# Samples' state products on two row quarters of the array, with their x rows spread by DMA

## The chip, the cores and the metric

The kernel runs on one core of one Trainium2 chip. Its time is the device time of one execution in microseconds (us); where several executions are given, the time is their median. The engines are named as the profile names them: PE is the matrix engine (PEld its loading of weights), DVE the vector engine, ACT the scalar engine, POOL the general-purpose engine, SP the engine that here only issues DMAs.

## The reference

The program is one inference step of a one-layer decoder. A layer has a mixer (a chunked gated MLP beside a Mamba-2 state-space model, SSD) and a convolutional feed-forward net. It works on 256 tokens of a new sequence (the prompt) and on 8 other sequences (the samples) of 8 new tokens each, 320 tokens in all. The part that the change touches is the samples' recurrence:

```
h_t = exp(dt_t a) h_{t-1} + dt_t x_t B_t^T,   y_t = h_t C_t
states = jnp.einsum("bcsgn,bcsgr,bcsgrp->bcgrpn", bc, decay_states, xdt)
...
ssm_state_sample  (DEPTH, DEC_BATCH, SSM_HEADS, SSM_HEAD_DIM, SSM_STATE)
```

There are 32 heads of 64 channels in 4 groups (8 heads each); a group shares B and C, which have 128 state entries. For each of the 8 samples and each of the 4 groups, the new state (128 x 512 numbers: state entries by the 8 heads' channels) is the old one, shrunk by a factor per head, plus the product of B (8 tokens x 128) with the decayed x (8 tokens x 512).

## The kernel before

All large products are projections: weights of 128 x 1024 numbers (a slab, 512 KB) come from memory by SP's DMAs, ACT rounds them to a high part `whi`, DVE subtracts that to get a low part `wlo`, and PE makes three products for each 128 x 128 block (`accumulate`, lines 131 to 137): high with high, high weights with the low part of the data, low weights with the high part. The moving side is always the 320 tokens. Both parts have the type fp32r, a rounded fp32.

The SSD work is cut into small steps. `ssd(g)` (from line 896) is a generator for group g = 0 to 3. A planner (`tick`, `advance`, lines 147 to 175) calls its next step between slabs of the projections, after a number of products that the step itself asked for with `yield`. So the SSD's matmuls stand in PE's order between slabs, at places fixed when the program is built; for groups 0 to 3 that is the stretch from about 415 to 800 us. The small matmuls write into a ring of four PSUM banks, `misc`.

The samples are handled in two halves, i = 0, 1 of four sequences each (32 tokens), and for each group in these steps:

- `fourfold` (line 427) makes on ACT `x4`, a copy of the samples' x with each half repeated four times along the tokens. `x_of_samples` (line 932) transposes it on PE, four transposes for each half, so that 128 rows hold 32 tokens four times over. `ps_x` are the two results.
- `samples_split` (line 938) multiplies by dt times the decay (`times`, DVE), ACT rounds the product into `xsp`, and DVE replaces rows 64 to 127 by what the rounding left over. `samples_rows` (line 944) takes other rows of the same transposes for the outputs y.
- `bsp` holds B in the same manner: four copies of 32 tokens, two of them high parts and two low parts, so that the sum over 128 rows gives all four products of high and low parts.
- `picked` (line 992) makes for each i of 0 to 3 on ACT a masked copy `bm` of `bsp`, in which only the rows of the i-th sequence of each half are kept; the mask is `bsel`.
- `shrunk` (line 997) multiplies the old states by their factor on POOL. `grown` (line 1003) makes, for the i-th sequence of each half h, one product of `bm[:, h]` with `xsp[:, h]` over all 128 rows (128 x 512), and DVE adds it to the state. `end` (line 1024) does that and stores the state. `ends` says in which steps: 2, 5, 7 and 10; for group 3 the last one is done behind all projections of the mixer (line 1125).

Thus there are 4 groups x 4 values of i x 2 halves = 32 of these products, in 16 pairs. PE's products for the state that goes in (`with_c`, `ps_yo`) and for the outputs (`products`, `y_ps`) use parts of the array, 32 or 64 of its columns side by side, by `tile_position`; the products of `grown` use it whole.

Of the kernel before, what the change touches and what calls it, by code (L numbers as in the profile page):

```python
# [33 lines left out]
def hybrid_step(  # L34
# [37 lines left out]
    bd2 = cp.tile([P, P], F32, name="bd2")  # L72
    bsel = cp.tile([P, 4], F32, name="bsel")
    upper_s = cp.tile([P, NS], F32, name="upper_s")
# [3 lines left out]
    def masks():  # L78
        make_upper_triangular(nc, upper, 1.0, diag=True)
        make_lower_triangular(nc, later, 1.0, diag=False)  # L80
        make_block_diagonal(nc, bd2, TS)

        for r in range(4):
            rs = slice(32 * r, 32 * r + 32)
            pool.tensor_copy(bsel[rs], bd2[rs, rs].rearrange("p (b t) -> p b t", b=4)[:, :, 0])
# [340 lines left out]

    def fourfold(out, x, i):

        act.copy(out.rearrange("p k (q t) -> p k q t", q=4), x[:, :, NP + 32 * i:NP + 32 * i + 32].unsqueeze(2).to_broadcast([P, 4, 4, 32]))
        return out  # L430

    with ExitStack() as mctx:
# [68 lines left out]
        def steps():  # L501
# [82 lines left out]
            act.activation(dec.rearrange("p c h -> p (c h)"), ps_dec[:, :H5], AF.Exp)  # L584
            dve.tensor_tensor(out=dt[:, 3:5], in0=dt[:, 3:5], in1=dec[:, 3:5], op=ALU.mult)

            sp.dma_start(tote, tot_d.unsqueeze(0).broadcast_to([P, NH, NB]))
# [3 lines left out]
        with tc.tile_pool(name="gp", bufs=1) as gp:  # L591
# [252 lines left out]
            for g in range(4):  # L844
                res = []
                mix = gate_mix(g, uf, res)
                bg.append(mix)
                if g < 3:
                    uf = gate_up(g + 1)
                    if g == 2:  # L850
                        b4 = [[tp.tile([P, NT], F32, tag="pv", name="b4", bufs=4)[:, :256] for _ in range(2)] for _ in range(2)]
                        for i in range(2):
                            o = NP + 32 * i
                            for h in range(2):
                                pool.dma_start(b4[i][h], b_d[o:o + 32, 256 * h:256 * h + 256].unsqueeze(0).broadcast_to([4, 32, 256]))
                    finish(mix)
                    chunk_out(w_out, g, *res, g == 0)
# [4 lines left out]
        with tc.tile_pool(name="sd", bufs=1) as sd:  # L862
# [3 lines left out]
            shared = op.tile([P, NT + NS + 2 * P], F32, tag="dtf", name="cb_cms", bufs=1)  # L866
            cb, cms = shared[:, :NT + NS], shared[:, NT + NS:].rearrange("p (b i) -> p b i", b=NB)
            pool.tensor_copy(cb[:NS, :NS], ident[:NS, :NS])
# [12 lines left out]
            def load_state(g, i):  # L881

                st = [sd.tile([P, 512], F32, tag="st", name="st", bufs=6) for _ in range(2)]
                for h in range(2):
                    sp.dma_start(st[h], state_ssm[4 * h + i, g])
                return st
# [9 lines left out]
            def ssd(g):  # L896
# [16 lines left out]
                for h in range(2):  # L913
                    sp.dma_start(st3[h], state_ssm[4 * h + 3, g])
# [16 lines left out]

                def x_of_samples(i):
                    ps = misc("xt_ps")
                    for j in range(4):
                        by_token(ps[:, P * j:P * j + P], x4[:, i, P * j:P * j + P], 0)
                    return ps

                def samples_split(i, ps):
                    xq = sd.tile([P, 512], F32, tag="xde", name="xq", bufs=2)
                    times(xq, ps, 3 + i)  # L940
                    act.copy(xsp[:, i], xq)
                    dve.tensor_tensor(out=xsp[64:, i], in0=xq[64:], in1=xsp[64:, i].bitcast(F32), op=ALU.subtract)

                def samples_rows(i, ps):
                    for r in range(2):
                        at = slice(64 - 64 * r + 32 * i, 96 - 64 * r + 32 * i)
                        times(xdt[at, 2, 256 * r:256 * r + 256], ps[at, 256 * r:256 * r + 256], 2, at, slice(4 * r, 4 * r + 4))

# [28 lines left out]

                ps_x = [x_of_samples(i) for i in range(2)]
                ps_s = misc("s1_ps")
# [4 lines left out]
                def with_c(i, st):  # L984

                    for r in range(2):
                        for h in range(2):
                            row = 64 * r + 32 * h
                            pe.matmul(ps_yo[row:row + 32, :256], cms[:, 4 * h + i, :], st[h][:, 256 * r:256 * r + 256],  # L989
                                      start=i == 0, stop=i == 3, tile_position=(0, row))  # L990

                def picked(i):
                    bm = sd.tile([P, 2, P], F32R, tag="bm", name="bm", bufs=2)
                    act.activation(bm, bsp[:, :, bs].bitcast(F32), AF.Copy, scale=bsel[:, i:i + 1])
                    return bm

                def shrunk(i, st):
                    with first():
                        for h in range(2):
                            pool.tensor_tensor(out=by_head(st[h]), in0=by_head(st[h]),  # L1000
                                               in1=tote[:, h0:h0 + 8, 4 * h + i:4 * h + i + 1].to_broadcast([P, 8, 64]), op=ALU.mult)

                def grown(st, bm):
                    for h in range(2):
                        ps = misc("up_ps")
                        made = pe.matmul(ps, bm[:, h], xsp[:, h], start=True, stop=True)  # L1006
                        with first():
                            dve.tensor_tensor(out=st[h], in0=st[h], in1=ps, op=ALU.add)
                    return made.ins

                def store_state(i, st, by=act):
                    for h in range(2):
                        by.dma_start(o_ssm_s[4 * h + i, g], st[h])

# [6 lines left out]

                bms = {}

                def end(i, by=act):
                    made = grown(sts[i], bms.pop(i))
                    store_state(i, sts[i], by)
# [56 lines left out]
                ends = {2: 0, 5: 1, 7: 2, 10: 3}  # L1083
                picks = {0: (0, 1), 2: (2,), 5: (3,)}
                shrinks = {0: 0, 2: 1, 5: 2, 8: 3}
# [4 lines left out]
                for n in range(13 - e):  # L1090
                    if n == 0:
                        samples_split(1, ps_x[1])
                    if n == 1:
                        for i in range(2):
                            samples_rows(i, ps_x[i])
# [3 lines left out]
                    for i in picks.get(n, ()):  # L1099
                        bms[i] = picked(i)  # L1100
                    if n in (6, 12 - e):
# [431 lines left out]
```

## Time and profile before

| | |
|---|---|
| time, median of 3 runs | 1751.21 us (1750.23 to 1751.52) |
| time of the profiled execution | 1750.2 us |
| its span, first to last instruction | 1748.5 us |
| granted PE clock | 0.999 |
| PE / PEld / DVE / ACT / POOL busy | 1740.9 / 1720.8 / 1181.3 / 822.2 / 316.8 us |
| DMA | 302.54 MB, 173 GB/s on average |

"Busy" for PE counts matmuls, which are pipelined: the next one starts while the one before still drains, so what a matmul costs is the time from its start to the next one's start (its slot), not its duration. A row of the timeline gives the start, the duration of the row's instructions together, the engine, the line, the operation, what it writes and reads, the part of the array (rows*columns), the moving data's shape, and how many instructions the row merges. An fp32 matmul stands as two instructions, one of fp32r and a transpose as one.

### The profile page before, as it was taken

The numbers are of one execution on the slowest core, as the hardware profiler recorded it, in microseconds if no ns is written. First come the engines' busy times: TensorE is split into PE (matmuls) and PEld (weight loads), VectorE is DVE, ScalarE is ACT, GpSimd is POOL, SyncE is SP. The second block draws the span as 40 slices with busy tenths as digits, with TensorE's granted clock in tenths as the row PEclk, the third lists the DMA queues.
The fourth block names the chain that finished last, engine by engine and source line by source line (L and its number), as shares of the span: only waits on it lengthen the run. The fifth ranks groups of instructions, "written<-read, shape, count | busy, mean of one in ns | idle before, by whom it ended". The sixth has DMA issues, their size and how long they took to land.

```text
span 1748.5 us, 31128 instructions
## 1 busy us (share of the span) xinstructions
PE 1740.9 (100%) x12075; PEld 1720.8 (98%) x12075; DVE 1181.3 (68%) x2015; ACT 822.2 (47%) x1202; POOL 316.8 (18%) x682
## 2 busy tenths in 40 slices
PE   9999999999999999999999999999999999999998
PEld 9999999999999999999999999999999999999997
DVE  7558864667969787778855566565657565656577
ACT  6344544334656565646545434343434343333345
POOL 2532230000423323111210101010201010101002
PEclk9999999999999999999999999999999999999999
DMA  8786565556576676664655555455554545555543
GB/s 262 223 233 182 183 176 157 154 166 195 189 227 206 198 232 194 213 191 151 190 156 152 154 148 157 146 155 150 155 150 149 155 149 149 157 149 155 146 159 109
DMA packets 227747, 302.54 MB, mean 173 GB/s; under 512 B 21392, under 2 KB 152080, under 8 KB 227408
## 3 DMA queue, kind: packets, MB, share of 16 engines
q1 hardware_dynamic: 210976, 272.42, 51.8%
q0 software_dynamic: 6176, 13.87, 2.6%
q10 hardware_dynamic: 10448, 14.26, 2.3%
q8 instruction: 95, 1.56, 0.4%
q14 instruction: 52, 0.43, 0.1%
HBM read 280.54 MB, written 19.69 MB: 172 GB/s over the span
## 4 chain that ended last, share of the span: by engine, by line
PE 98%; DVE 1%; ACT 1%; issue 0%; POOLq 0%; ACTq 0%
PE ps L134 21%; PE ps L135 20%; PE ps L136 20%; PE pd L134 10%; PE pd L136 10%; PE pd L135 10%; PE y_ps L1070 1%; PE ps_v L135 1%; PE ps_v L134 1%; PE ps_v L136 1%; PE yo_ps L989 0%; PE up_ps L1006 0%; PE sg L812 0%; PE xt_ps L412 0%; DVE wlo L124 0%; ACT whi L123 0%
## 5 line engine op out<-in xcount | busy, mean ns | idle before, releaser
L124 DVE TENSOR_TENSOR wlo<-wraw,whi 128x1024 fp32r<-128x1024 f32 (+2 forms) x480 | 583.0, 1215 | 416.7 <-ACT whi L123 414.0
L123 ACT CAST whi<-wraw 128x1024 fp32r<-128x1024 f32 (+2 forms) x479 | 495.7, 1035 | 688.7 <-PE ps L135 393.9
L134 PE MATMUL ps<-h_hi,whi 128*128 128x320 f32 x2428 | 750.1, 309 | 0.0
L135 PE MATMUL ps<-h_lo,whi 128*128 128x320 f32 x2428 | 748.5, 308 | 0.0
L136 PE MATMUL ps<-h_hi,wlo 128*128 128x320 f32 x2428 | 747.9, 308 | 0.0
L134 PEld LDWEIGHTS ps<-h_hi,whi 128*128 128x128 f32 x2428 | 455.5, 188 | 3.1 <-issue 1.8
L135 PEld LDWEIGHTS ps<-h_lo,whi 128*128 128x128 f32 x2428 | 455.7, 188 | 0.4
L136 PEld LDWEIGHTS ps<-h_hi,wlo 128*128 128x128 f32 x2428 | 455.5, 188 | 0.0
L136 PE MATMUL pd<-fhi,wlo 128*128 128x320 f32 x704 | 217.0, 308 | 0.0
L135 PE MATMUL pd<-flo,whi 128*128 128x320 f32 x704 | 217.0, 308 | 0.0
L134 PE MATMUL pd<-fhi,whi 128*128 128x320 f32 x704 | 217.0, 308 | 0.0
L134 PE MATMUL pd<-ohi,whi 128*128 128x320 f32 x448 | 138.8, 310 | 0.0
L136 PE MATMUL pd<-ohi,wlo 128*128 128x320 f32 x448 | 138.3, 309 | 0.0
L135 PE MATMUL pd<-olo,whi 128*128 128x320 f32 x448 | 138.3, 309 | 0.0
L136 PEld LDWEIGHTS pd<-fhi,wlo 128*128 128x128 f32 x704 | 132.1, 188 | 0.0
L134 PEld LDWEIGHTS pd<-fhi,whi 128*128 128x128 f32 x704 | 132.1, 188 | 0.0
L135 PEld LDWEIGHTS pd<-flo,whi 128*128 128x128 f32 x704 | 132.1, 188 | 0.0
L1318 POOL COPY ptf<-pad 128x2 f32<-128x2 f32 x88 | 21.0, 238 | 602.2 <-DVE pad L1306 601.5
L247 DVE TENSOR_TENSOR acc_ffn<-acc_ffn,pd 128x320 f32<-128x320 f32 (+1 forms) x161 | 77.1, 479 | 29.3 <-PE pd L136 28.0
L134 PEld LDWEIGHTS pd<-ohi,whi 128*128 128x128 f32 x448 | 84.1, 188 | 0.7
L135 PEld LDWEIGHTS pd<-olo,whi 128*128 128x128 f32 x448 | 84.1, 188 | 0.3
L136 PEld LDWEIGHTS pd<-ohi,wlo 128*128 128x128 f32 x448 | 84.1, 188 | 0.0
(342 smaller groups left out, 1728.4 us busy)
## 6 DMA issues: line engine op xcount, KB each, us to landing
wraw<-in_ffn_w_up SPq DMA_DIRECT2D x176, 512.0 KB, 3.7
wraw<-in_w_in SPq DMA_DIRECT2D x132, 512.0 KB, 4.0
wraw<-in_ffn_w_down SPq DMA_DIRECT2D x88, 512.0 KB, 3.4
wraw<-in_w_out SPq DMA_DIRECT2D x64, 512.0 KB, 3.5
st<-in_state_ssm SPq DMA_DIRECT2D x40, 256.0 KB, 4.3
out_ssm_state_sample<-st ACTq DMA_DIRECT2D x30, 256.0 KB, 3.0
cs<-dacs_d SPq DMA_DIRECT2D x16, 320.0 KB, 4.8
wraw<-in_w_in SPq DMA_DIRECT2D x12, 384.0 KB, 4.1
```

The costliest lines, as they stand in the source:

```text
L123: rounded[:] = [act.copy(hi, raw).ins]
L124: dve.tensor_tensor(out=lo, in0=raw, in1=hi.bitcast(F32), op=ALU.subtract)
L134: pe.matmul(ps, whi, xhi, start=first, stop=False)
L135: pe.matmul(ps, whi, xlo, start=False, stop=False)
L136: last_made[0] = pe.matmul(ps, wlo, xhi, start=False, stop=last).ins
L247: added_last[:] = [dve.tensor_tensor(out=acc[:, nb, ts], in0=acc[:, nb, ts], in1=ps[:, ts], op=ALU.add).ins]
L1070: pe.matmul(ps[64 * i:64 * i + 64, cols], w(hl), x(hl, m, cpx), tile_position=(0, 64 * i), **flags)
L1318: pool.tensor_copy(ptf[:, k, :], pad[:, 256:258])
```

## The change

The rows of `bsp` and `xsp` are put in another order. Before, the 128 rows of a half were four blocks, each with all 32 tokens; now they are 32 runs of four, each run for one token: two copies of high parts and two of low parts of B (`odd`, `sign` tell which rows), high and low parts of x in turn. So the 32 rows of a quarter of the array belong to one sequence of 8 tokens, and a product for that sequence needs only its quarter.

- The masks `bsel`, the masked copies `bm` and `picked` are gone (16 ACT instructions of 128 x 256).
- `grown` makes its two products first, each on 32 rows, on two different quarters ((i + h) mod 4), and then the two additions. `seq(h, i)` renumbers the sequences to fit; the loads and stores of states follow it.
- The fourfold copy is gone (8 ACT copies). `x_of_samples` makes four transposes straight from `xs`, of 64 columns each (all samples once), in place of eight of 128.
- `samples_split` works once on 64 rows: a multiplication on DVE, a rounding on ACT into rows 0 to 63 of the new tile `x_parts`, a subtraction on DVE into rows 64 to 127. `x_parts` takes a buffer of the ring `xde`.
- New: `strips` fills `xsp` from `x_parts` by four DMAs within SBUF for each group, each of 64 rows of 2 KB and repeating a row twice: the high parts from ACT's queue, the low parts from POOL's. The shrinking of the states 1 to 3 is ordered behind POOL's two DMAs (`issue_after(filled[1])`).
- `samples_rows` takes two DVE instructions of 64 rows in place of four of 32, in step 0 instead of 1.
- In `b_of_samples`, once: four ACT instructions with a scale per row, and eight DVE instructions over all rows in place of eight over 32 rows. The DMAs that bring B repeat each token four times instead of the block.
- Small things at the start: two DVE instructions make `odd` and `sign`; four POOL copies that made `bsel` are gone; one POOL copy joins the decays of the two halves in `dt`.

In PE's order every matmul keeps its place. In group 0, before (the rows are engine order, not time; `ps` and `pd` are slab products):

```order
L136 MATMUL ps_3_4579<-h_hi,wlo 128x320
L412 MATMUL xt_ps<-ident,x_4628 128x128 x8
L980 MATMUL s_ps<-xde,btok 128x512
L989 MATMUL yo_ps<-st,cb_cms 32x256 x12
...
L136 MATMUL pd_5_5091<-ohi,wlo 128x320
L1006 MATMUL up_ps<-xsp,bm 128x512 x2
L134 MATMUL pd_6_5123<-ohi,whi 128x320
```

and now:

```order
L134 MATMUL ps_3_4579<-h_hi,wlo 128x320
L933 MATMUL xt_ps<-ident,xs 64x128 x4
L989 MATMUL s_ps<-xde,btok 128x512
L998 MATMUL yo_ps<-st,cb_cms 32x256 x12
...
L134 MATMUL pd_5_5078<-ohi,wlo 128x320
L1012 MATMUL up_ps<-xsp,bsp 128x512 x2
L132 MATMUL pd_6_5108<-ohi,whi 128x320
```

Four transposes are left of eight, and the pair `up_ps` reads `bsp` itself; nothing else moved on PE.

On POOL, around the fill of group 1, before (`st` are states being shrunk, `xde` and `cpx` decayed copies for the outputs):

```order
L1120 TENSOR_TENSOR s_5793<-s_5793,dec 128x512
L928 TENSOR_TENSOR xde<-xdt,dec 128x512
L1000 TENSOR_TENSOR st<-st,tote 128x512 x6
L928 TENSOR_TENSOR xde<-xdt,dec 128x512
L1050 TENSOR_TENSOR cpx<-cpx,cT 128x256
```

and now:

```order
L1121 TENSOR_TENSOR s_5768<-s_5768,dec 128x512
L926 TENSOR_TENSOR xde<-xdt,dec 128x512
L1004 TENSOR_TENSOR st<-st,tote 128x512 x2
L948 DMA xsp<-x_parts 64x1x512 x2
L1004 TENSOR_TENSOR st<-st,tote 128x512 x4
L926 TENSOR_TENSOR xde<-xdt,dec 128x512
L1056 TENSOR_TENSOR cpx<-cpx,cT 128x256
```

The two DMAs stand between the first and the second pair of shrunk states; four of the six, `xde` and `cpx` come behind them.

The diff, cut to its core:

```diff
-                                pool.dma_start(b4[i][h], b_d[o:o + 32, 256 * h:256 * h + 256].unsqueeze(0).broadcast_to([4, 32, 256]))
+                                pool.dma_start(b4[i][h], b_d[o:o + 32, 256 * h:256 * h + 256].unsqueeze(1).broadcast_to([32, 4, 256]))
...
-                        act.copy(out, raw)
-                        for rs in (slice(32, 64), slice(96, P)):
-                            dve.tensor_tensor(out=out[rs], in0=raw[rs], in1=out[rs].bitcast(F32), op=ALU.subtract)
+                        act.activation(out, raw, AF.Copy, scale=sign)
+                        for k in range(2):
+                            dve.scalar_tensor_tensor(out=out[:, :, k], in0=raw[:, :, k], scalar=odd, in1=out[:, :, k].bitcast(F32),
+                                                     op0=ALU.mult, op1=ALU.add)
+            def seq(h, i):
+                return 4 * h + (i + h) % 4
...
-                x4 = sd.tile([P, 2, 512], F32, tag="xsp", name="x4", bufs=1)
-                for i in range(2):
-                    fourfold(x4[:, i].rearrange("p (k n) -> p k n", n=P), xs, i)
...
-                def x_of_samples(i):
+                def x_of_samples():
                     ps = misc("xt_ps")
                     for j in range(4):
-                        by_token(ps[:, P * j:P * j + P], x4[:, i, P * j:P * j + P], 0)
+                        pe.transpose(ps[:NS, P * j:P * j + P], xs[:, j, NP:NT], ident)
                     return ps
 
-                def samples_split(i, ps):
+                def samples_split(ps):
                     xq = sd.tile([P, 512], F32, tag="xde", name="xq", bufs=2)
-                    times(xq, ps, 3 + i)
-                    act.copy(xsp[:, i], xq)
-                    dve.tensor_tensor(out=xsp[64:, i], in0=xq[64:], in1=xsp[64:, i].bitcast(F32), op=ALU.subtract)
+                    parts = sd.tile([P, 512], F32R, tag="xde", name="x_parts", bufs=2)
+                    lower = slice(0, NS)
+                    times(xq[lower], ps[lower], 3, lower)
+                    act.copy(parts[lower], xq[lower])
+                    dve.tensor_tensor(out=parts[NS:], in0=xq[lower], in1=parts[lower].bitcast(F32), op=ALU.subtract)
+                    return parts
+
+                def strips(parts, half):
+                    for i in range(2):
+                        o = NS * half + 32 * i
+                        made = (pool if half else act).dma_start(xsp[half::2, i].bitcast(F32),
+                                                                 parts[o:o + 32].bitcast(F32).unsqueeze(1).broadcast_to([32, 2, 512]))
+                    return made.ins
...
-                def picked(i):
-                    bm = sd.tile([P, 2, P], F32R, tag="bm", name="bm", bufs=2)
-                    act.activation(bm, bsp[:, :, bs].bitcast(F32), AF.Copy, scale=bsel[:, i:i + 1])
-                    return bm
...
-                def grown(st, bm):
+                def grown(i, st):
+                    up = []
                     for h in range(2):
-                        ps = misc("up_ps")
-                        made = pe.matmul(ps, bm[:, h], xsp[:, h], start=True, stop=True)
+                        rs = slice(32 * ((i + h) % 4), 32 * ((i + h) % 4) + 32)
+                        up.append(misc("up_ps"))
+                        made = pe.matmul(up[h], bsp[rs, h, bs], xsp[rs, h], start=True, stop=True, tile_position=(rs.start, 0))
+                    for h in range(2):
                         with first():
-                            dve.tensor_tensor(out=st[h], in0=st[h], in1=ps, op=ALU.add)
+                            dve.tensor_tensor(out=st[h], in0=st[h], in1=up[h], op=ALU.add)
...
-                samples_split(0, ps_x[0])
+                x_parts = samples_split(ps_x)
+                filled = [strips(x_parts, half) for half in range(2)]
...
                     if n in shrinks:
-                        shrunk(shrinks[n], sts[shrinks[n]])
+                        with tc.issue_after(filled[1]) if n else nullcontext():
+                            shrunk(shrinks[n], sts[shrinks[n]])
```

More of the change, by code (lines that the diff above doesn't have):

```diff
@@ L72, in hybrid_step @@
     bd2 = cp.tile([P, P], F32, name="bd2")
-    bsel = cp.tile([P, 4], F32, name="bsel")
+    odd = cp.tile([P, 1], F32, name="odd")
+    sign = cp.tile([P, 1], F32, name="sign")
     upper_s = cp.tile([P, NS], F32, name="upper_s")
@@ L81, in masks @@
         make_block_diagonal(nc, bd2, TS)
-        for r in range(4):
-            rs = slice(32 * r, 32 * r + 32)
-            pool.tensor_copy(bsel[rs], bd2[rs, rs].rearrange("p (b t) -> p b t", b=4)[:, :, 0])
         for r in range(2):
@@ L867, in hybrid_step @@
             cb, cms = shared[:, :NT + NS], shared[:, NT + NS:].rearrange("p (b i) -> p b i", b=NB)
+            dve.tensor_reduce(out=odd, in_=ident.rearrange("p (t d h) -> p d t h", d=2, h=2)[:, 1], axis=mybir.AxisListType.XY, op=ALU.add)
+            dve.tensor_scalar(out=sign, in0=odd, scalar1=-2.0, scalar2=1.0, op0=ALU.mult, op1=ALU.add)
             pool.tensor_copy(cb[:NS, :NS], ident[:NS, :NS])
@@ L930, in decayed, with samples_rows @@
                     return xde
-                def x_of_samples(i):
+                def x_of_samples():
                     ps = misc("xt_ps")
                     for j in range(4):
-                        by_token(ps[:, P * j:P * j + P], x4[:, i, P * j:P * j + P], 0)
+                        pe.transpose(ps[:NS, P * j:P * j + P], xs[:, j, NP:NT], ident)
                     return ps
-                def samples_split(i, ps):
+                def samples_split(ps):
                     xq = sd.tile([P, 512], F32, tag="xde", name="xq", bufs=2)
-                    times(xq, ps, 3 + i)
-                    act.copy(xsp[:, i], xq)
-                    dve.tensor_tensor(out=xsp[64:, i], in0=xq[64:], in1=xsp[64:, i].bitcast(F32), op=ALU.subtract)
-                def samples_rows(i, ps):
+                    parts = sd.tile([P, 512], F32R, tag="xde", name="x_parts", bufs=2)
[10 more added lines that the diff above has]
+                    return made.ins
+                def samples_rows(ps):
                     for r in range(2):
-                        at = slice(64 - 64 * r + 32 * i, 96 - 64 * r + 32 * i)
-                        times(xdt[at, 2, 256 * r:256 * r + 256], ps[at, 256 * r:256 * r + 256], 2, at, slice(4 * r, 4 * r + 4))
+                        at, hs = slice(NS - NS * r, P - NS * r), slice(256 * r, 256 * r + 256)
+                        dve.tensor_tensor(out=by_head(xdt[at, 2, hs]), in0=by_head(ps[:NS, hs]),
+                                          in1=dt[:NS, 2, h0 + 4 * r:h0 + 4 * r + 4].unsqueeze(2).to_broadcast([NS, 4, 64]), op=ALU.mult)
                 for c in range(2):
@@ L976, in ssd @@
                 yield 48, 72
-                ps_x = [x_of_samples(i) for i in range(2)]
+                ps_x = x_of_samples()
                 ps_s = misc("s1_ps")
@@ L988, in with_c @@
                             row = 64 * r + 32 * h
-                            pe.matmul(ps_yo[row:row + 32, :256], cms[:, 4 * h + i, :], st[h][:, 256 * r:256 * r + 256],
+                            pe.matmul(ps_yo[row:row + 32, :256], cms[:, seq(h, i), :], st[h][:, 256 * r:256 * r + 256],
                                       start=i == 0, stop=i == 3, tile_position=(0, row))
-                def picked(i):
-                    bm = sd.tile([P, 2, P], F32R, tag="bm", name="bm", bufs=2)
-                    act.activation(bm, bsp[:, :, bs].bitcast(F32), AF.Copy, scale=bsel[:, i:i + 1])
-                    return bm
                 def shrunk(i, st):
@@ L1091, in ssd @@
                     if n == 0:
[L1092 to L1095, printed above, removed]
+                        samples_rows(ps_x)
                         yo_to_xdt()
```

18 lines of the change are left out of this document (6 added, 12 removed).

## The prediction

> **What bounds the kernel now.** I read the engines' busy times first, then the chain of work that ended last, then the table of who waited for whom, and last PE's timeline at the places that the change touches. From the page:
>
> ```profile
> PE 1740.9 (100%) x12075; PEld 1720.8 (98%) x12075; DVE 1181.3 (68%) x2015; ACT 822.2 (47%) x1202; POOL 316.8 (18%) x682
> ...
> PE 98%; DVE 1%; ACT 1%; issue 0%; POOLq 0%; ACTq 0%
> ```
>
> PE is busy all the time and is 98% of the chain. All that PE waited for in 1748.5 us (engine, line, what it waited for, us in total, times, longest):
>
> ```profile
> PE early L69 <- DVE ones L65: 1.1, 1, 1.1
> PE both L1423 <- ACT f_tok L1421: 1.0, 1, 1.0
> ```
>
> One wait is at the start, one at the end; between them PE runs through its fixed order without a gap. So a matmul is worth its slot, the time from its start to the next start, and work of ACT, DVE, POOL or the DMAs is worth nothing, unless PE comes to wait for it. The forecast is therefore a sum of PE slots in 16 pairs of state products and 4 sets of transposes.
>
> **The pairs before.** PE's timeline at the first pair (start, duration, engine, line, operation, part of the array, shape, how many):
>
> ```profile
> 459.84 0.31 PE L134 MATMUL pd<-ohi,whi 128*128 128x320 f32 x1
> 459.99 0.31 PE L135 MATMUL pd<-olo,whi 128*128 128x320 f32 x1
> 460.14 0.31 PE L136 MATMUL pd<-ohi,wlo 128*128 128x320 f32 x1
> 460.29 0.62 PE L1006 MATMUL up_ps<-xsp,bm 128*128 128x512 f32 x2
> 460.75 0.30 PE L134 MATMUL pd<-ohi,whi 128*128 128x320 f32 x1
> 460.89 0.31 PE L135 MATMUL pd<-olo,whi 128*128 128x320 f32 x1
> ```
>
> Slab products start every 0.147 us. From 460.14 to 460.89 are 0.75 us with the pair, and would be 0.29 without: a pair costs 0.46 us, 0.23 for each product of 512 columns.
>
> **The pairs after.** Each product now takes 32 of the 128 rows, so the array changes from whole to row quarters and back 16 times. The trace has no row quarter, but it has column parts and one half of the rows. Column parts, at group 0, with the sample transposes ahead of them:
>
> ```profile
> 435.22 0.31 PE L136 MATMUL ps<-h_hi,wlo 128*128 128x320 f32 x1
> 435.37 1.03 PE L412 MATMUL xt_ps<-ident,x 128*128 128x128 f32 x8
> 436.24 1.02 PE L980 MATMUL s_ps<-xde,btok 128*128 128x512 f32 x2
> ...
> 436.67 0.59 PE L980 MATMUL s_ps<-xde,btok 128*128 128x512 f32 x1
> 437.20 1.93 PE L989 MATMUL yo_ps<-st,cb_cms 128*32 128x256 f32 x32
> 439.06 0.41 PE L134 MATMUL ps<-h_hi,whi 128*128 128x320 f32 x1
> 439.31 0.31 PE L135 MATMUL ps<-h_lo,whi 128*128 128x320 f32 x1
> 439.46 0.31 PE L136 MATMUL ps<-h_hi,wlo 128*128 128x320 f32 x1
> ```
>
> (436.67 is the second of the two `s_ps` instructions, shown alone.) And half of the rows, 64*128, in the steps near 232 us:
>
> ```profile
> 232.60 0.39 PE L556 MATMUL dec_ps<-sp_e,ones 128*128 128x32 f32 x2
> 232.71 0.28 PE L556 MATMUL dec_ps<-sp_e,ones 128*128 128x32 f32 x1
> 232.92 0.29 PE L558 MATMUL dec_ps<-sp_e,sums_of 64*128 64x32 f32 x1
> ```
>
> What a change of parts costs:
>
> - Going in: the second `s_ps` instruction holds PE for 0.53 us (436.67 to 437.20), the first for 0.43: 0.10 us. For rows the same: 0.21 (232.71 to 232.92) against 0.11 for the like instruction before it, 0.10 us.
> - Going out: the 32 `yo_ps` run four side by side, so in 8 turns, each half as long as the 512 columns of `s_ps`: 8 x 0.215 = 1.72. From 437.20 to 439.06 are 1.86; 0.03 of the rest are the first weights (32 columns), about 0.10 the way out.
> - The first slab product afterwards holds PE for 0.25 us (439.06 to 439.31), the next for 0.147: 0.10 us. It lasts 0.41 in place of 0.31: its weights, elsewhere loaded under the product before, are loaded in the open.
> - The pair's own weights are loaded in the open too. How long, tell the weight loads (mean ns last):
>
> ```profile
> L1006 PEld LDWEIGHTS up_ps<-xsp,bm 128*128 128x128 f32 x32 | 5.4, 188 | 0.0
> L558 PEld LDWEIGHTS dec_ps<-sp_e,sums_of 64*128 64x128 f32 x4 | 0.5, 186 | 0.0
> L989 PEld LDWEIGHTS yo_ps<-st,cb_cms 128*32 128x32 f32 x128 | 3.7, 109 | 5.1 <-PE xt_ps L412 3.0
> L412 PEld LDWEIGHTS xt_ps<-ident,x 128*128 128x128 f32 x32 | 3.7, 141 | 0.0
> ```
>
> Half of the rows takes as long as all (186 and 188), a quarter of the columns much less (109): the time goes by columns, and the pair keeps its 128. So 0.10 us again; the two quarters load at the same time, as `yo_ps` shows for columns.
>
> The two streams run side by side: 0.22 us (between half of 0.43 and 0.23). A pair after: 0.10 in, 0.10 weights, 0.22 stream, 0.10 out, 0.10 for the next slab's weights, 0.62 us. Against 0.46: **+0.16 us, times 16 = +2.6 us**. The stream saved is smaller than the two changes of parts.
>
> TensorEngine Tiling (Array Packing) in the Trainium skill says, under Key Properties, that a change of the tiling mode, not of the tile alone, drains TensorE; the trace agrees, with 0.10 us on each side. By that page's Theoretical Speedup alone (an estimate: two tiles, two times) the pairs would give -3.7 us; with its drain, at the trace's prices, they give the +2.6.
>
> Bounds: if row quarters cost nothing to enter and leave, a pair is 0.23 us, -3.7 in all; if the quarters load one after the other, 0.72 us, +4.2; if they also stream one after the other, 0.84 us, +6.1. I take the row of 64*128, the nearest in kind, which shows the change at its full price.
>
> **The transposes.** Eight in 0.87 us (435.37 to 436.24), 0.109 each; four go, 0.44 us. But the four that stay have 64 columns of weights, so they run on half of the columns (128*64), between two works on the whole array. That adds 0.10 in, 0.03 for their first weights (a transpose's load is short, 141 ns for 128 columns), 0.10 out, and 0.10 for the weights of `s_ps`, now in the open: 0.33. **-0.11 us, times 4 = -0.4 us.** Bounds: -1.7 without any change of parts; +1.3 if a transpose on half of the columns takes two instructions, as every other fp32 product does.
>
> **Sum: +2.2 us.** The profiled execution took 1750.2 us, 1748.5 span and 1.7 around it, so it would take 1752.4. It lies 1.0 below the median of the runs shown, to which the change is added: **1753.4 us**. A measurement of this kernel tells about 0.2%, 3.5 us, from no change; this is +0.13%.
>
> **Off the path.** ACT loses the masked copies and the fourfold copies, DVE half of the splits; the tables of instructions by form (count, busy us, mean ns) for 415 to 800 us, and two rows of the whole span:
>
> ```profile
> L994 ACT ACTIVATE bm<-bsp,bsel 128x256 fp32r<-128x256 f32 x16 | 8.0, 505 | 1.0 <-DVE ssq L330 0.7 <-issue 0.2
> L429 ACT COPY x<-xs 128x512 f32<-128x512 f32 x8 | 4.8, 618 | 1.7 <-DVE wlo L124 1.2 <-DVE st L1008 0.6
> L942 DVE TENSOR_TENSOR xsp<-xq,xsp 64x512 fp32r<-64x512 f32 x8 | 7.4, 934 | 0.2
> ...
> L310 DVE TENSOR_REDUCE small<-turned 128x10 f32<-128x320 f32 x4 | 1.9, 477 | 0.1
> L259 DVE TENSOR_SCALAR small<-small 128x10 f32<-128x10 f32 x4 | 0.7, 172 | 0.1
> ```
>
> About 16 us of ACT and DVE work go in this stretch, worth nothing, as PE did not wait for it. `odd` and `sign` add at most 0.65 us to DVE at the start (the last two rows), 0 on PE, which waits there only for `ones`. The new wait is for the fill. It is tightest in group 1; POOL's and PE's timelines there, POOL's four issues of B's copies and their time to landing:
>
> ```profile
> 519.65 7.26 POOL L1000 TENSOR_TENSOR st<-st,tote 128x512 f32<-128x512 f32 x6 [11.56 <-PE yo_ps L989]
> ...
> 531.44 0.63 PE L1006 MATMUL up_ps<-xsp,bm 128*128 128x512 f32 x2
> ...
> 553.03 0.39 PE L1006 MATMUL up_ps<-xsp,bm 128*128 128x512 f32 x1
> ...
> 382.16 0.73 POOL L855 DMA_DIRECT2D b<-b_d  x1 [7.40 <-ACT uf L391]
> 383.89 0.70 POOL L855 DMA_DIRECT2D b<-b_d  x1 [1.00 <-ACT uf L391]
> ...
> b<-b_d POOLq DMA_DIRECT2D x4, 128.0 KB, 4.7
> ```
>
> POOL is through with the first two of the six states at 519.65 + 2 x 1.21 = 522.1, issues its second DMA 1.73 later, and that lands 4.7 after: 528.5. The first pair of group 1 starts at 531.44, 2.9 us later, so 0 us. Queued behind the DMAs on POOL are the states of the next pairs, 3.5 us later (526.9 becomes 530.4); the second pair comes at 553.03. ACT's two issues stand ahead of its next slab's rounding, but ACT has just lost more. The fills move 16 x 128 KB, 2.1 MB on slabs of 512 KB, and no slab was waited for.
>
> **The rivals.**
>
> 1. Faster: row quarters change without a drain, all else as summed: -3.7 - 0.4 = -4.1, 1747.1 us. For it speaks that 32 rows are far from what the trace holds; against it, that 64 rows paid the full 0.10. It decides when the four surcharges of a pair, 0.40 by the rows, fall below 0.04 in all; below 0.26 the time is under the one before. Chance 0.08.
> 2. Slower: the quarters do not run side by side: loads one after the other, +1.6 on the forecast, 1755.0; streams too, +3.5, 1756.9. Only column parts show it here, four at a time. Chance 0.13.
> 3. Slower: the transposes take two instructions each on half of the columns: +1.7, 1755.1. Every fp32 product on column parts in this trace is two, and no transpose runs there. It decides (over 3.5 us) from 12 of the 16 transposes on, 0.109 us each on top of the forecast. TensorEngine Tiling (Array Packing) in the Trainium skill, Gotcha 2, lists the transpose mode for fp32 input among what column tiling excludes; no run here shows it yet, and by it the sum would be +3.9. Chance 0.20; with rival 2 together 0.03, 1756.7.
> 4. Slower: the fill comes late; if it lands over 2.9 us later than reckoned, PE stands still for the rest, in groups 1 and 3 alike; 2 us in each gives 1757.4. Chance 0.06.
>
> **How the numbers follow.** The forecast has 0.50. Faster by over 0.2% (below 1747.7) is rival 1 and little else: 0.09. Slower by over 0.2% (above 1754.7) are most of rivals 2 and 4, a little over half of rival 3, which lies on the line, and the tail of the forecast: 0.31. Within: 0.60. The range leaves out rival 1 and the far ends: 1751.0 to 1757.0.
>
> **What will show it.** At a pair, two `up_ps` on 32*128 that start within 0.01 us, the next slab product about 0.42 us after them, and the one behind that 0.25 later; rival 1 shows 0.15 there, rival 2 a second start 0.1 or 0.2 us behind the first. Four `xt_ps` on 128*64 for each group, or eight (rival 3). PE's table of waits without a row for `up_ps`; a row there is rival 4. The prediction is wrong if PE's slots at the pairs differ from 0.62 us by more than a tenth, or if PE waits anywhere else.

## The result

| | before | after |
|---|---|---|
| time, median of 19 runs each | 1750.97 us | 1753.39 us |
| lowest and highest | 1749.68, 1751.71 | 1750.88, 1754.64 |
| time of the profiled execution | 1750.2 | 1751.36 |
| its span | 1748.5 | 1749.3 |

The ratio is 1.0015, 95% interval 1.0009 to 1.0021: slower by 2.4 us, less than the 0.2% taken for no change. The two spans differ by 0.8 us only. The kernel after was profiled a second time, in an execution of 1754.51 us, and that shows where the rest comes from. The first profile is read first. Its page, busy times and chain:

```profile
PE 1741.8 (100%) x12059; PEld 1716.2 (98%) x12059; DVE 1173.9 (67%) x2001; ACT 809.2 (46%) x1174; POOL 320.9 (18%) x687
...
PE 99%; DVE 0%; ACT 0%; issue 0%; ACTq 0%
```

PE is the bound as before, with 16 instructions less. PE's timeline at the first pair of group 0:

```profile
459.57 0.31 PE L133 MATMUL pd<-olo,whi 128*128 128x320 f32 x1
459.72 0.31 PE L134 MATMUL pd<-ohi,wlo 128*128 128x320 f32 x1
459.96 0.50 PE L1012 MATMUL up_ps<-xsp,bsp 32*128 32x512 f32 x2
460.39 0.41 PE L132 MATMUL pd<-ohi,whi 128*128 128x320 f32 x1
460.64 0.31 PE L133 MATMUL pd<-olo,whi 128*128 128x320 f32 x1
```

From 459.72 to 460.64 are 0.92 us, two slab slots (0.29) of which would be there without the pair: 0.63. The product ahead holds PE for 0.24 in place of 0.147 (the way in), the pair itself for 0.43; the first slab product behind holds it for 0.25 and lasts 0.41 (its weights in the open). The transposes of group 0, with what stands around them:

```profile
435.24 0.31 PE L134 MATMUL ps<-h_hi,wlo 128*128 128x320 f32 x1
435.38 0.60 PE L933 MATMUL xt_ps<-ident,xs 128*64 128x128 f32 x4
435.82 1.02 PE L989 MATMUL s_ps<-xde,btok 128*128 128x512 f32 x2
436.77 1.93 PE L998 MATMUL yo_ps<-st,cb_cms 128*32 128x256 f32 x32
```

The trace marks them as 128*64, and yet nothing around them is longer: 0.14 us from the slab product to the first transpose, 0.44 for four (0.109 each), 0.95 for the two `s_ps`, as before (436.24 to 437.20 was 0.96). So four transposes less are worth the whole 0.44 us in each group. By PE's slots the pairs cost 16 x 0.16 = +2.6 us (added up over all 16 in the two traces: 9.92 us, before 7.30) and the transposes give -1.7: +0.9 us, which agrees with the spans.

### The profile page after: what moved, and what is told of

Read it like the earlier page. It is cut to its first block, busy times and chain, and to the rows that moved or that the text cites. A ratio compares the mean times of both kernels' runs of the same rounds, so it can differ in the third digit from the quotient of the medians.

```text
span 1749.3 us, 31077 instructions
## 1 busy us (share of the span) xinstructions
PE 1741.8 (100%) x12059; PEld 1716.2 (98%) x12059; DVE 1173.9 (67%) x2001; ACT 809.2 (46%) x1174; POOL 320.9 (18%) x687
## 4 chain that ended last, share of the span: by engine, by line
PE 99%; DVE 0%; ACT 0%; issue 0%; ACTq 0%
PE ps L132 21%; PE ps L134 20%; PE ps L133 20%; PE pd L132 10%; PE pd L134 10%; PE pd L133 10%; PE y_ps L1076 1%; PE ps_v L132 1%; PE ps_v L134 1%; PE ps_v L133 1%; PE yo_ps L998 0%; PE sg L806 0%; PE up_ps L1012 0%; PE early L69 0%; PE fin_ps L1145 0%; PE xt_ps L410 0%
```

## The second profile: what the first did not show

> The changed kernel as it is, profiled once more. Read from its first profile, PE's slots give +2.5 us for the pairs and -1.7 us for the transposes (four for each group, 0.109 us each, without the 0.33 us of a change of parts that was forecast), +0.8 us together, which is also the difference of the two spans, 1749.3 against 1748.5. But the medians stand 2.4 us apart. Theory (a wait): in most executions PE waits 1.5 to 2 us for something that the first profile found in time; then a profile with a span near 1751.3 has a row in the table of PE's waits, or a slab product that starts late. Rival (longer slots): no wait, and the slots of the slab products are longer by 1.5 us over some 11,300 of them, 0.13 ns each. Second rival: the median is near 1751.5 this time, and the 1.6 us were the chip of the first runs.

Measured: 1754.01 us median of 11 runs (1751.47 to 1754.76), ratio 1.0018 (1.0009 to 1.0027). The profile of the execution of 1754.51 us, span 1752.5, has a row of waits that the first does not have, and PE's timeline shows the two places:

```profile
PE pd L134 <- DVE wlo L122: 2.3, 2, 1.7
```

```profile
449.68 0.31 PE L133 MATMUL pd<-olo,whi 128*128 128x320 f32 x1
451.73 0.41 PE L134 MATMUL pd<-ohi,wlo 128*128 128x320 f32 x1 [1.74 <-DVE wlo L122]
...
458.72 0.31 PE L133 MATMUL pd<-olo,whi 128*128 128x320 f32 x1
459.62 0.42 PE L134 MATMUL pd<-ohi,wlo 128*128 128x320 f32 x1 [0.59 <-DVE wlo L122]
```

The slots are 2.05 and 0.90 us instead of 0.147: 2.65 us lost, and 0.2 more in the slots behind them, of the 3.2 us between the two spans. DVE's low parts of the weights (`wlo`) come late. DVE and POOL in this execution:

```profile
439.14 1.95 DVE L122 TENSOR_TENSOR wlo<-wraw,whi 128x1024 fp32r<-128x1024 f32 x1 [1.25 <-ACT whi L121]
441.11 1.44 DVE L942 TENSOR_TENSOR x_parts<-xq,x_parts 64x512 fp32r<-64x512 f32 x1
442.58 0.86 DVE L1026 TENSOR_TENSOR xdt<-yo_ps,ed 64x256 f32<-64x256 f32 x2
443.45 6.68 DVE L978 TENSOR_TENSOR cb_cms<-cmask,cT 128x128 f32<-128x128 f32 x2
450.06 0.48 DVE L1065 TENSOR_TENSOR cs<-cs,cb_cms 128x320 f32<-128x320 f32 x1
450.46 1.21 DVE L122 TENSOR_TENSOR wlo<-wraw,whi 128x1024 fp32r<-128x1024 f32 x1
```

```profile
442.85 1.10 POOL L948 DMA_DIRECT2D xsp<-x_parts  x2 [0.84 <-DVE x_parts L942]
443.97 4.11 POOL L1004 TENSOR_TENSOR st<-st,tote 128x512 f32<-128x512 f32 x4
448.05 1.03 POOL L926 TENSOR_TENSOR xde<-xdt,dec 128x512 f32<-128x512 f32 x1
449.05 0.73 POOL L1056 TENSOR_TENSOR cpx<-cpx,cT 128x256 f32<-128x256 f32 x1
```

`cb_cms` are two masked copies of C for the next group. Over the span each takes (ns, least, median, most):

```profile
L978 DVE TENSOR_TENSOR cb_cms<-cmask,cT x8: 280/681/6476, 237.7 to 604.8; 128x128 f32<-128x128 f32 x8
```

The first of these two took 6.48 us, the second 0.28 (the text on record for the copies by POOL, below, calls the long one the second; alone, the row of the first is this):

```profile
443.45 6.48 DVE L978 TENSOR_TENSOR cb_cms<-cmask,cT 128x128 f32<-128x128 f32 x1
```

It begins 0.06 us after the start of POOL's second DMA (443.40), 0.5 us ahead of POOL's first state, and ends when POOL has finished six products in a row, of which the states ran at full pace (1.03 us each). The weights behind the copies on DVE were due at 449.8, and DVE began them at 450.46. In the first profile the same instructions of DVE and POOL:

```profile
441.16 1.36 DVE L978 TENSOR_TENSOR cb_cms<-cmask,cT 128x128 f32<-128x128 f32 x2
442.45 1.35 DVE L1065 TENSOR_TENSOR cs<-cs,cb_cms 128x320 f32<-128x320 f32 x1
443.72 2.08 DVE L122 TENSOR_TENSOR wlo<-wraw,whi 128x1024 fp32r<-128x1024 f32 x1
```

```profile
441.13 1.11 POOL L948 DMA_DIRECT2D xsp<-x_parts  x2
442.26 5.73 POOL L1004 TENSOR_TENSOR st<-st,tote 128x512 f32<-128x512 f32 x4
```

Here DVE came 2.3 us earlier, at the start of POOL's two DMAs in place of 0.6 us behind it, and had nearly done its copies (0.29 and 1.15 us) when POOL's states began; from then on the two took turns (both slower: 1.43 us for a state, 2.08 for `wlo`). What set DVE back in the other execution is the load of the sums that ACT waits for; ACT's timelines, first and second profile:

```profile
435.94 0.42 ACT L1055 ACTIVATE cpx<-cs 128x256 f32<-128x256 f32 x1 [1.68 <-DMA cs<-dacs_d]
```

```profile
437.75 0.42 ACT L1055 ACTIVATE cpx<-cs 128x256 f32<-128x256 f32 x1 [3.26 <-DMA cs<-dacs_d]
```

A load that lands 1.8 us later moves ACT's next rounding, with it DVE's `wlo` (1.6 us later, and 1.95 us long in place of 1.21), and DVE's copies then meet the start of POOL's second row of states. That row has a start only since the change: before, POOL's six states of a group stood in one row (437.93 to 446.74 us), and DVE's two copies, at its end, took 2.20 us:

```profile
437.93 8.81 POOL L1000 TENSOR_TENSOR st<-st,tote 128x512 f32<-128x512 f32 x6 [0.29 <-PE yo_ps L989]
445.75 2.20 DVE L969 TENSOR_TENSOR cb_cms<-cmask,cT 128x128 f32<-128x128 f32 x2
```

The long copy does not need so late a load. In the profile of four products at once, an experiment told below, ACT started only 0.4 us later than in the first profile (436.36), and yet the first copy stood 6.49 us:

```profile
441.56 1.11 POOL L948 DMA_DIRECT2D xsp<-x_parts  x2 [0.85 <-DVE x_parts L942]
442.16 6.69 DVE L978 TENSOR_TENSOR cb_cms<-cmask,cT 128x128 f32<-128x128 f32 x2
442.69 4.12 POOL L1004 TENSOR_TENSOR st<-st,tote 128x512 f32<-128x512 f32 x4
```

The two profiles with the long copy have this in common: POOL had finished its first two states and waited for DVE's `x_parts` (0.84 and 0.85 us), and the copies came 0.60 us behind the start of its two DMAs. In the first profile POOL's states ended last, and the DMAs began together with the copies.

Of the 30 runs of the kernel after, 24 took 1753.1 to 1754.8 us, and 6 took 1750.9 to 1752.2, as the first profile did. One of the 24 was profiled; that the others lost their time in the same way is inferred from their times.

SBUF — State Buffer in the Trainium skill, under Who interferes with whom, says that a DVE instruction with two inputs in SBUF contends with a POOL instruction that reads SBUF; under SBUF: two separate sides it adds that whichever starts first has the shared ports for its whole instruction. The trace agrees with the contention (2.08 us in place of 1.21 for `wlo`), but not with the rest: here DVE's copy started 0.5 us ahead of the first state and was the one that waited, for six instructions, 6.48 us, not for one.

## The experiments

**Two edits against the lost turn.** The copies of C by POOL:

```diff
-                    dve.tensor_tensor(out=cms[:, 4 * hb:4 * hb + 4], in0=cmask[:, 4 * hb:4 * hb + 4],
+                    pool.tensor_tensor(out=cms[:, 4 * hb:4 * hb + 4], in0=cmask[:, 4 * hb:4 * hb + 4],
...
```

> The changed kernel with one edit: the two masked copies of C for the next group are made by POOL in place of DVE. In the second profile of the changed kernel the second of these copies on DVE lasted 6.48 us beside POOL's unbroken row of four states and two more products, DVE's next rounded weights came late, and PE waited 1.74 and 0.59 us for them; in its first profile the same copy took 0.68 us and PE did not wait. Theory (a lost turn between DVE and POOL): without these copies on DVE nothing stands there when POOL begins its row, the waits go, and the median is that of the executions without the wait, about 1751.4, with all runs within 1.5 us of each other. Rival (DVE is simply short of time at that place, as ACT starts late behind a load, and any operation of DVE that meets POOL's row is held as long): another operation of DVE shows the 5 to 6 us, PE waits as before, and the median stays at 1753.5.

The fill's lower half by SP, with POOL's states in one row again:

```diff
-                        made = (pool if half else act).dma_start(xsp[half::2, i].bitcast(F32),
+                        made = (sp if half else act).dma_start(xsp[half::2, i].bitcast(F32),
...
-                        with tc.issue_after(filled[1]) if n else nullcontext():
+                        with nullcontext():
```

> The changed kernel with POOL's two fill DMAs issued by SP, so that POOL's six states of a group stand in one row again, as before the change. Theory (the gap that the two DMAs make lets DVE's copies of C run up against the start of POOL's second row): POOL is in the middle of its row when DVE comes to the copies, they alternate as in the kernel before (about 1.1 us for each copy), no wait for the rounded weights: 1751.4. Rival: the copies lose their turn wherever they meet a row of POOL: 6 us and more for one, 1753.5 or later. Cost of the edit itself: SP waits 1 to 2 us for the lower parts with the next slab behind it; if that shows, a row of PE's waits names a slab's load.

Measured: 1751.46 us (1750.69 to 1752.28) and 1751.61 us (1750.65 to 1751.94); none of these 22 runs is over 1752.3, and both profiles have only the two old waits of PE, at the start and at the end. DVE and POOL with the fill by SP:

```profile
442.44 2.27 DVE L978 TENSOR_TENSOR cb_cms<-cmask,cT 128x128 f32<-128x128 f32 x2
```

```profile
437.92 7.70 POOL L1004 TENSOR_TENSOR st<-st,tote 128x512 f32<-128x512 f32 x6
```

The copies meet POOL's row in its middle and take turns, as before the change. Each edit alone, one on DVE's side and one on POOL's, brings the time of the executions without the wait. So the wait is the meeting of these two, and it costs 1.8 to 2.6 us in the median (1.3 to 2.4 if each kernel is set against the kernel before as timed beside it). That ACT's late start alone isn't enough shows in an experiment told below (the sums one step later): there DVE was as late, and the copies were POOL's; no wait followed at 449.

```profile
439.15 1.95 DVE L122 TENSOR_TENSOR wlo<-wraw,whi 128x1024 fp32r<-128x1024 f32 x1 [1.29 <-ACT whi L121]
```

**The transposes' half alone.** The pairs whole again, masked by ACT:

```diff
+                def picked(i):
+                    bm = sd.tile([P, 2, P], F32R, tag="bm", name="bm", bufs=2)
+                    act.activation(bm, bsp[:, :, bs].bitcast(F32), AF.Copy, scale=bsel[:, i:i + 1])
+                    return bm
...
-                        made = pe.matmul(up[h], bsp[rs, h, bs], xsp[rs, h], start=True, stop=True, tile_position=(rs.start, 0))
+                        made = pe.matmul(up[h], bms[i][:, h], xsp[:, h], start=True, stop=True)
```

> The transposes' half of the change alone: x of the samples transposed once and its rows filled by DMA as in the changed kernel, but each state product again on the whole array with B masked by ACT, as before. The theory of slots: a pair costs 0.46 us again in place of 0.62, so 2.5 us under the changed kernel; against the kernel before 16 transposes less, 0.109 each, -1.7 us: about 1749.3. If the 1.6 us that the medians lie above the slots belong to the fill by DMA, 1750.9, and PE's table of waits or a late slab product shows it; if they belong to the row quarters, 1749.3. Had the forecast's change of parts at the transposes been paid, -0.4: 1750.6.

Measured: 1749.40 us (1748.49 to 1749.60), ratio to the kernel before 0.9992 (0.9984 to 1.0001). PE's timeline at the first pair:

```profile
459.41 0.31 PE L137 MATMUL pd<-ohi,wlo 128*128 128x320 f32 x1
459.56 0.62 PE L1019 MATMUL up_ps<-xsp,bm 128*128 128x512 f32 x2
460.02 0.31 PE L135 MATMUL pd<-ohi,whi 128*128 128x320 f32 x1
460.17 0.31 PE L136 MATMUL pd<-olo,whi 128*128 128x320 f32 x1
```

0.76 less 0.29 is 0.47 us for a pair, against 0.63 on quarters. This kernel lies 2.1 us under the kernel after without its wait (1751.46), the price of 16 changes of parts: 2.6 by the slots. The transposes' gain is real, all of it but some tenths: -1.3 against the kernel before, -1.7 by the slots, with one new wait of 0.3 us for `olo` near 546 in its profile. Here too POOL's row has the gap and DVE makes the copies, and none of the 11 runs is long: in the profile the copies come in the middle of POOL's second row (442.18 us; the row begins at 441.79) and take turns, 1.15 us each. So the gap alone does not make the wait.

**Products on the transposes' columns.** The same four transposes as plain products with the identity:

```diff
-                        pe.transpose(ps[:NS, P * j:P * j + P], xs[:, j, NP:NT], ident)
+                        pe.matmul(ps[:NS, P * j:P * j + P], xs[:, j, NP:NT], ident, start=True, stop=True)
```

> The changed kernel with its 16 transposes of the samples' x as plain fp32 products with the identity, on the same 64 columns. An fp32 product is two instructions here: eight for each group, +0.44 us. Theory: a transpose does not change the array's parts but a product on 64 columns does (B times C on 128*64 pays 0.10 us on its way in after the product before it): +0.33 us more for each group, +3.1 us in all on the changed kernel, 1756.5. Rival: 64 columns that start at column 0 never cost a change, whatever runs on them: +1.7 us, 1755.1.

Measured: 1754.66 us (1754.15 to 1756.23). PE's timeline:

```profile
435.39 0.31 PE L134 MATMUL ps<-h_hi,wlo 128*128 128x320 f32 x1
435.63 1.09 PE L933 MATMUL xt_ps<-ident,xs 128*64 128x128 f32 x8
436.64 1.12 PE L989 MATMUL s_ps<-xde,btok 128*128 128x512 f32 x2
437.70 1.93 PE L998 MATMUL yo_ps<-st,cb_cms 128*32 128x256 f32 x32
```

From the slab product to `yo_ps` are 2.31 us; with transposes 1.53. Of the 0.78 more, 0.44 are four more instructions (at the transposes' 0.109 us each), and 0.34 are put down to the change of parts: 0.10 before the first (0.24 in place of 0.14), 0.14 more within and behind the eight (1.01 against 8 x 0.109), 0.11 in `s_ps` (1.06 against 0.95). This is the 0.33 that was forecast for the transposes: the forecast was right for products, while transposes pay nothing. The time lies 3.2 us over the kernel without the wait (3.1 reckoned). 1756.5 was reckoned from the median with the wait, and the profile of this kernel does not have it: there the copies begin with POOL's first DMA (441.89 and 441.85 us), as in the first profile. Whether two of the 11 runs (1755.74 and 1756.23 us) had it was not settled.

**Four products at once.** Two steps' pairs on all four quarters:

```diff
-                return 4 * h + (i + h) % 4
+                return 4 * h + (i + 2 * h) % 4
...
-                ends = {2: 0, 5: 1, 7: 2, 10: 3}
+                ends = {5: (0, 1), 10: (2, 3)}
```

> The changed kernel with two steps' four state products on the four quarters at once: 9 changes of parts for row quarters in place of 16. If a change costs what the prediction reckoned (0.10 in, 0.10 for the pair's weights, 0.22 stream, 0.10 out, 0.10 for the next weights) and four quarters run side by side as two do, 7 times 0.62 us go, 4.3 us: about 1749.0, under both kernels. Rival: four quarters share something that two do not (weights or streams one after the other): at 0.10 to 0.32 us more for each of the 7 merged turns the gain is 2 to 3.6 us. Second rival: DVE takes four sums in one go and a product waits for a bank of PSUM; then PE's waits have a row.

Measured: 1751.81 us (1749.67 to 1752.81). PE's timeline at such a place, and PE's waits beside the two of every run:

```profile
492.20 0.31 PE L134 MATMUL ps<-h_hi,wlo 128*128 128x320 f32 x1
492.45 0.51 PE L1012 MATMUL up_ps<-xsp,bsp 32*128 32x512 f32 x4
492.88 0.42 PE L132 MATMUL ps<-h_hi,whi 128*128 128x320 f32 x1
493.14 0.31 PE L133 MATMUL ps<-h_lo,whi 128*128 128x320 f32 x1
```

```profile
PE pd L133 <- DVE olo L398: 1.4, 1, 1.4
PE pd L134 <- DVE wlo L122: 1.1, 2, 0.6
...
PE ps L132 <- DVE acc_mix L245: 0.7, 2, 0.4
```

Four products cost 0.65 us, two cost 0.63 (both read from rows rounded to 0.01): quarters load and stream side by side, and what a pair pays is the change of parts. 1749.0 was forecast; the 4.3 us are saved at the pairs and taken back by waits for DVE: 3.2 us by this table, and about 4.6 in PE's slots (4.05 at the five waits, 0.5 in the slots behind them, whose weights are loaded in the open). The two waits for `wlo` stand behind the long copy shown above. With the copies of C on POOL:

> The kernel with four state products on the four quarters at once, and the copies of C on POOL. In the profile of the four at once PE waited 0.70 and 0.76 us at 449.6 and 457.4 (the rounded weights behind a copy of C of 6.49 us), 1.06 near 579 and 1.53 at 645.6 us, 3.2 us in all beyond the two waits of every run. Theory: the first two waits go with the copies, the other two stay: 1752.0 less 1.5, about 1750.5. If the copies were only a symptom, 1751.8 as before.

Measured: 1750.42 us (1748.98 to 1752.28), as forecast: the waits for `wlo` went, the other two stayed. Three edits were to end those. The first takes priority from DVE's sums of the second state and has POOL issue its stores, the second puts these sums and stores one step later, the third does that and leaves group 2 as it was:

> As the one with four at once and the copies of C on POOL, and DVE's sums of the second state without priority over the rounding of weights, its two stores issued by POOL in place of ACT. The wait of 1.06 us near 579 stood behind four sums in a row (2.47 us of DVE) and four stores in a row (2.2 us of ACT). Theory: it goes, 1749.5; if the wait at 645.6 goes as well (it has POOL's states beside DVE's scaling), 1748. The slots alone, without any wait, give the first profile's 1751.36 less 7 x 0.62: 1747.0.

> Four state products on the four quarters at once and the copies of C on POOL, with DVE's two sums and the two stores of the second state one step later, so that no four sums and no four stores stand in a row. With the four in a row PE waited 0.4 to 1.1 us near 578 and 1.3 to 1.5 us near 645. Theory: both waits come from the rows of four; they go, and the time is that of the slots alone, 1747.0. Rival: near 645 DVE's scaling beside POOL's states is late by the later place of the first pair itself, so that wait stays: 1748.5; and if a bank of PSUM is held too long PE waits at the products behind: a row for y_ps.

> The same, but group 2 (the one with the wait near 645) keeps its four single pairs at their old places: 11 changes of parts in place of 9. Slots: the changed kernel without waits, 1751.4, less 5 x 0.62: 1748.3. If the wait near 645 belongs to the moved pairs of group 2 it is gone here; if it comes from elsewhere, 1749.7.

Measured: 1751.28 (1748.94 to 1755.03), 1751.43 (1750.03 to 1754.16), 1750.47 us (1748.60 to 1752.22). All three were misses in time. In the first two the wait for `olo` (1.3 and 1.5 us, near 644) stays, so it is not the row of four sums that makes it; the wait for `acc_mix` stays as well (0.5 and 0.4 us), and the first has a new one of 0.4 at `up_ps`. The wait for `olo` belongs to the moved pairs of group 2: with those at their old places it is gone from there, as forecast, and the profile of that execution (1749.14 us) has only 0.3 us for `olo` near 741 and 0.2 more at the end. But the median of that kernel lies 2.2 us over the 1748.3 of its slots, and what its longer runs wait for was not settled. None of these beat the half change.

**The fastest by slots and waits.** The transposes' half alone and the copies of C on POOL:

> The transposes' half of the change, the pairs on the whole array with B masked as before, and the copies of C on POOL: the version that by the runs so far should be the fastest. Slots: the kernel before less 16 x 0.109. The profile of the same version with the copies on DVE had 1749.5 with one wait of 0.3 us for DVE near 546. Theory: what is off PE's path moves nothing any more, so 1749.0 to 1749.5, under both kernels, with all runs within 1.5 us. Rival: the copies on POOL push POOL's states back and a sum on DVE, and with it a product's bank, comes late: 1750 or more.

Measured: 1749.29 us (1748.52 to 1750.87), ratio to the kernel before 0.9994 (0.9985 to 1.0003), in the range that was forecast, but with runs 2.4 us apart, not 1.5. The two versions with the half change are the only ones with a median more than 1 us under the kernel before; each interval still takes in no change.

## Why the prediction was right or wrong

The time came out as forecast, 1753.39 against 1753.4, but two steps of the prediction failed in opposite directions. That the number agrees so closely is luck.

1. *A pair from 0.46 to 0.62 us, +2.6 us.* Right: 0.63 measured (0.43 from the pair's start to the next product, where 0.42 were reckoned, and 0.10 on each side), 0.47 for a whole pair with the same data, +2.6 us by the slots. The half of the rows (64*128) was the right row to take for quarters.
2. *The transposes, -0.11 us each group, -0.4 in all.* Mis-sized: -0.44 each group, -1.7 in all, which the prediction had as the lower bound. Its step "so they run on half of the columns (128*64), between two works on the whole array" took a price from products; the transposes do not pay it, products in the same place pay 0.34.
3. *ACT's and DVE's work is worth nothing, and what is queued behind POOL's two DMAs comes 3.5 us later without harm.* This failed, by about +2 us in the median. The prediction followed the moved work to PE by one way, the fill to the next pair, in group 1 where it is tightest. It didn't ask what the gap in POOL's row does to DVE: in group 0 a copy on DVE meets the start of the second row, stands 6.5 us, and the rounding of weights behind it makes PE wait. The delay on POOL itself was over-reckoned: its two DMAs hold it for 1.1 us, not 3.5. By its own test ("if PE waits anywhere else") the prediction is wrong there.
4. *The fill lands in time.* Right: PE has no row for `up_ps`.
5. *The rivals.* Row quarters without a drain: no, 0.24 on the way in. Quarters one after the other: no, even four run together. Two instructions for each transpose: no, four for each group. TensorEngine Tiling (Array Packing) in the Trainium skill, Gotcha 2, spoke for it; the trace shows fp32 transposes on 64 columns in one instruction each, without a change of parts.

So +2.2 was forecast as +2.6 - 0.4, and it is +2.6 - 1.7 + about 2 us of a wait that no rival had (2.4 us in all in the first set of runs, 3.3 in the second).

## What to carry to other kernels

Here a change of the array's parts for one pair of short products cost 0.16 us more than the two products on the whole array; only four products that shared one change cost less in PE's slots (0.65 us against two pairs' 0.94). Where PE is the bound, work moved on POOL must be followed to DVE too, not only to its own consumers: put the timelines of the two engines side by side at every place where the moved work starts or ends. And profile an execution that is as long as the median before explaining a difference of a few us: the first profile here was one of the short ones.

## What was not expected of the hardware

- An fp32 transpose of 64 columns, marked 128*64 in the trace, starts 0.14 us behind a product on the whole array and leaves the next one as it was; plain fp32 products in the place of the four cost, beyond their own slots, 0.34 us more.
- Row quarters behave as column parts do: two products together last 0.50 us and four 0.51, and four cost what two cost.
- A DVE instruction of 0.28 us stood 6.48 us beside six POOL instructions in a row, while in other executions the two engines took turns after each instruction. What decides between the two was not settled. In the two profiles with the long copy, the first copy begins 0.06 and 0.04 us after the start of POOL's second DMA, 0.5 us ahead of the first state. In the first profile and with the plain products it begins together with POOL's first DMA (the copies take 0.29 and 1.15 us); in the others of DVE's copies shown it begins beside a row of states (1.1 to 1.2 us each).
